# A two-layer encoder on one core: the last round of the feed-forward's second product over all tokens, and un-normed features for layer 1

## The chip, the cores and the metric

The kernel runs on one core of a Trainium2 chip. The metric is the device time of one execution in microseconds (us), the median of several. Five engines work beside each other: TensorE (PE, with weight loads PEld), VectorE (DVE), ScalarE (ACT), GpSimd (POOL) and SyncE (SP), which issues the DMAs.

## The reference, cut to what matters

Two groups of tokens (1024 of a new stream and 64 of a running one) share all weights, so the kernel has T = 1088 columns. Layer 0 has mixers A and B, layer 1 has C and D; behind each stands a squared-ReLU MLP. What the change touches is the MLP's second product, the norm that opens layer 1, layer 1's mixer and the final norm:

```
def trunk(x, ...):                         # D_MODEL 1024, D_FF 4096, two layers
    for layer in range(2):
        h = rms_norm(x, norm_mix_g[layer])
        y = even_mixer(h) if layer == 0 else odd_mixer(h)
        x = x + y
        h = rms_norm(x, norm_ffn_g[layer])
        x = x + square(relu(h @ w_ff1[layer])) @ w_ff2[layer]
    return rms_norm(x, final_norm_g)

def rms_norm(x, g):  return x * rsqrt(mean(x * x) + EPS) * g

def odd_mixer(h):
    z = h @ w_in
    c_in = z[:, :512] * sigmoid(z[:, 512:1024])
    c = silu(layer_norm(causal_dwconv(c_in, 31 taps) + bias))
    gate_b, gate_c, xt = z[:, 1024:1536], z[:, 1536:2048], z[:, 2048:]
    d = gate_b * causal_dwconv(gate_c * xt, 3 taps)
    return concat(c, d) @ w_out
```

## The kernel before, in words

Features lie on the 128 partitions, tokens along the columns. x is eight tiles X of 128 x 1088. The tokens are cut into two halves c = 0 and c = 1 of NH = 544 columns, each of two quarters of NQ = 272. Every fp32 operand is split into a rounded high part and a remainder (`split`, lines 164 to 166: an ACT copy, then a DVE subtraction), and every product takes three matmuls.

**Feed-forward.** Both products of the MLP use seven products of 2 x 2 block matrices in place of eight. `form` (line 197) makes the seven weight forms of one block: one load into RAW, four sums on DVE (line 212), seven splits into slots W, of which there are six. `take` and `ahead` (lines 234 and 220) make forms ahead of their use, in the order of a plan. The hidden features are stored in DRAM as seven forms each (`hd`), and `Hidden.form` loads and splits them back into tiles FA (c = 0) and FB (c = 1), four each.

The second product goes in steps (`STEPS2`, lines 333 to 336): a step multiplies for output block j the hidden blocks lo to hi, seven forms f, for the halves in cs; `products` (line 782) issues 7 x 3 matmuls per hidden block and half, and line 878 adds each form's PSUM result into X. In the last round hidden blocks 12 + j to 15 are multiplied for j = 0 to 3 (4, 3, 2, 1 blocks wide), first for c = 1, all four j, then for c = 0, all four j again:

```
STEPS2 += [(j, 12 + j, 16, (), (c,)) for c in (1, 0) for j in range(4)]
```

So the weight forms of these four steps are loaded and made twice. In this round the updated X is squared on ACT (lines 885 and 888, one square tile `sq`) and summed on POOL into acc (line 889).

**Norm and layer 1.** When a half is done, `done(c)` appends its norm to `beside`, a list from which `aside` takes two pieces after each form. In layer 0 that is `norm1` (line 900): `rms_half` (line 297: two sums on PE, a reciprocal root on ACT, three DVE steps, lines 305 to 308), then for each of the eight tiles a store of x to DRAM, a product with gain and factor on DVE (line 908) and a split into tiles h. For c = 1 these run beside the matmuls of c = 0; for c = 0 beside the first projections, which `conv_pairs` (line 1014) therefore issues for c = 1 first: gates and GLU inputs of pair 0 and the gate of pair 1 for c = 1, then c = 0.

`project` (line 957) multiplies one 128-row block of the input projection for both halves, 48 matmuls a half, into one of two PSUM pairs. A gate is emptied by a sigmoid on ACT (line 998), a GLU input by a DVE product (line 1002). `conv` (line 1046) lists the 31 taps of each of four channel blocks for DVE (line 1074, accumulating in PSUM) or, all 31 of block 0 and 18 of block 2, for POOL (line 1063, with ACT products); `some` (line 948) releases them at fixed rates after each half-projection. `short_conv` (line 1093) does the same for mixer D: gate_c is copied by ACT (line 1101), gate_x is a DVE product (line 1105), two taps on DVE (line 1116), gate_b a DVE product (line 1123) and a split into dd. The order in which an engine runs its instructions is not the source's: the framework that builds the program orders them itself.

**The end.** For layer 1 `finish(c)` (line 1202) scales the eight tiles of a half on ACT (line 1208), does `rms_half`, multiplies by the factor on DVE or POOL (line 1213) and stores the output. The pieces of c = 1 run beside c = 0's matmuls.

Of the kernel before, what the change touches and what calls it, by code (L numbers as in the profile page):

```python
# [16 lines left out]
P = 128  # L17
# [39 lines left out]
def encoder(ctx, tc, ins, outs):  # L57
# [29 lines left out]
    RIGHT = {"P1", "P2", "t", "raw", "FA", "vr", "sq", "RAW", "e", "cin", "dd", "wide", "yt"}  # L87
    LEFT = {"Q1", "Q2", "FB", "vl", "h", "cc"}
# [108 lines left out]
    def form(key, blocks):  # L197
# [99 lines left out]
    def rms_half(c, t):  # L297

        ps = pair()
# [32 lines left out]

    STEPS2 = [(2, 0, 2, (2,)), (3, 0, 3, (3,)), (1, 0, 1, ()), (0, 0, 4, (4,))]
    STEPS2 += [((w - 4) % 4, w - 4, w, (w,)) for w in range(5, 16)]
    STEPS2 = [(*s, (0, 1)) for s in STEPS2]
    STEPS2 += [(j, 12 + j, 16, (), (c,)) for c in (1, 0) for j in range(4)]

    def plan_ff(layer):
# [5 lines left out]
        for s, (j, a, b, _, _) in enumerate(STEPS2):  # L344
            src = ins[f"wf2_{layer}"][j, :, :, a * P : b * P].rearrange("b p c -> p b c")
            for f in range(7):
                plan(("f2", layer, s, f), src, "form")
# [422 lines left out]
    def feed_forward(layer, done):  # L770
# [10 lines left out]

        def products(key, cs, n, rows):
# [5 lines left out]
            for f, (name, first) in enumerate(  # L788
# [4 lines left out]
                w = take((*key, f), 5)  # L793
                for c in cs:
                    ps = bank[name][:, c, :NQ]
                    for q in range(n):
                        lh, ll = w[:, 0, q * P : q * P + P], w[:, 1, q * P : q * P + P]
                        t = FF[c, rows[q]][:, PLACE[f]]
# [6 lines left out]
                aside(2)  # L805

        class Hidden:
# [5 lines left out]
            def form(self, f):  # L813
                t = self.buffer()
                dma.dma_start(out=t, in_=hd[self.i][f])
                for c in range(2):
                    to = FF[c, self.i % 4][:, PLACE[f]]
                    split(to[:, 0], to[:, 1], t[:, c * NQ : c * NQ + NQ])

        factor = acc.rearrange("p (c h t) -> p c h t", c=2, h=2)  # L820
        for s, (i, cs) in enumerate(STEPS1):
# [4 lines left out]
            for f, ps in products(("f1", layer, s), cs, 4, range(4)):  # L826
# [45 lines left out]
        for s, (j, lo, hi, make, cs) in enumerate(STEPS2):  # L872
            nxt = [Hidden(i) for i in make]
            for f, ps in products(("f2", layer, s), cs, hi - lo, [k % 4 for k in range(lo, hi)]):

                m, h = ((j, 0), (j + 4, 1), (j, 1), (j, 0), (j + 4, 1), (j, 1), (j + 4, 0))[f]
                t = xv[m][:, cs[0] : cs[-1] + 1, h]
# [447 lines left out]
```

## Time and profile before

| | |
|---|---|
| median of 3 runs | 2128.63 us (2127.48 to 2131.05) |
| the profiled execution | 2128.48 us, span in the trace 2126.7 us |
| mean granted PE clock | 0.978 |
| PE busy | 2012.8 us (95%) |
| DVE busy | 1687.0 us (79%) |
| ACT busy | 993.7 us (47%) |
| POOL busy | 276.6 us (13%) |

Times in the trace are counted from the span's start. A window's row gives the busy time of each engine in it with the number of its instructions in brackets; PEclk is the granted clock of TensorE as a share of full speed. A row of lines groups equal instructions: count, busy us, mean ns, then the engine's idle time ahead of them and what ended it.

### The profile page before, as it was taken

To read this page: it belongs to the slowest core of one execution; us is meant where nothing else is said; L and a number is where in the kernel's file an instruction comes from. 1 tells how busy PE (TensorE), PEld (TensorE's weight loads), DVE (VectorE), ACT (ScalarE), POOL (GpSimd) and SP (SyncE) were. 2 spreads that over 40 slices of the span, in tenths; PEclk is the share of its full clock that TensorE was granted. 3 is DMA by queue.
4 is the path that set the end of the run, shared out by engine and by line. 5 is a ranking of instruction groups with operands and counts; after the bars stand their busy time and mean duration, and the time that the engine had idled before them with its cause. 6 is when DMAs were issued, how large, how long until landed. Compare 5 with 4: busy or idle time off the path is not lost.

```text
span 2126.7 us, 38667 instructions
## 1 busy us (share of the span) xinstructions
PE 2012.8 (95%) x15212; PEld 1975.0 (93%) x15212; DVE 1687.0 (79%) x2855; ACT 993.7 (47%) x1836; POOL 276.6 (13%) x204
## 2 busy tenths in 40 slices
PE   7999998999998999997899999979999989999995
PEld 5799998999998999997899999979999989999984
DVE  7785789676769988889579967998676779888887
ACT  6233555444445444444454425664343454444453
POOL 5200110000000000002166750300000000000023
PEclk9999999999999999998999999999999999999997
DMA  4223224434347445422211141234434466444412
GB/s 151 71 62 103 85 94 145 159 125 160 126 167 248 152 133 155 134 88 97 98 50 43 31 104 61 90 105 144 152 141 143 146 209 191 151 136 153 128 56 99
DMA packets 128406, 259.83 MB, mean 122 GB/s; under 512 B 16928, under 2 KB 38560, under 8 KB 123616
## 3 DMA queue, kind: packets, MB, share of 16 engines
q1 hardware_dynamic: 128224, 257.37, 37.1%
q8 instruction: 119, 1.95, 0.4%
q14 instruction: 63, 0.52, 0.1%
HBM read 185.69 MB, written 71.63 MB: 121 GB/s over the span
## 4 chain that ended last, share of the span: by engine, by line
PE 74%; DVE 16%; ACT 3%; issue 3%; POOL 2%; DMA 2%; DVEq 0%; SPq 0%; ACTq 0%; POOLq 0%
PE pp L801 19%; PE pp L803 18%; PE pp L802 18%; PE pp L248 4%; PE pp L249 4%; PE pp L250 4%; DVE W L166 2%; PE ps L248 2%; DVE ps L1074 2%; PE ps L249 2%; PE ps L250 2%; DVE X L878 1%; DMA vr<-hd 1%; DVE FB L166 1%; DVE Wl L166 1%
## 5 line engine op out<-in xcount | busy, mean ns | idle before, releaser
L801 PE MATMUL pp<-FA,W 128*128 128x272 f32 x1792 | 526.2, 295 | 45.6 <-DVE X L878 28.6
L801 PE MATMUL pp<-FB,W 128*128 128x272 f32 x1792 | 520.4, 290 | 16.4 <-DVE W L166 10.8
L802 PE MATMUL pp<-FA,W 128*128 128x272 f32 x1792 | 522.8, 292 | 0.1
L803 PE MATMUL pp<-FA,W 128*128 128x272 f32 x1792 | 522.2, 292 | 0.0
L803 PE MATMUL pp<-FB,W 128*128 128x272 f32 x1792 | 515.4, 288 | 0.0
L802 PE MATMUL pp<-FB,W 128*128 128x272 f32 x1792 | 515.3, 288 | 0.0
L801 PEld LDWEIGHTS pp<-FA,W 128*128 128x128 f32 x1792 | 344.0, 192 | 55.1 <-DVE X L878 32.2
L801 PEld LDWEIGHTS pp<-FB,W 128*128 128x128 f32 x1792 | 337.8, 188 | 20.5 <-issue 9.3
L802 PEld LDWEIGHTS pp<-FA,W 128*128 128x128 f32 x1792 | 345.9, 193 | 0.6 <-DVE FA L166 0.5
L803 PEld LDWEIGHTS pp<-FA,W 128*128 128x128 f32 x1792 | 343.4, 192 | 0.0
L802 PEld LDWEIGHTS pp<-FB,W 128*128 128x128 f32 x1792 | 341.3, 190 | 0.0
L803 PEld LDWEIGHTS pp<-FB,W 128*128 128x128 f32 x1792 | 337.9, 189 | 0.0
L166 DVE TENSOR_TENSOR W<-RAW,W 128x512 fp32r<-128x512 f32 (+3 forms) x356 | 234.4, 662 | 55.6 <-ACT W L165 54.7
L165 ACT ACTIVATE W<-RAW 128x512 fp32r<-128x512 f32 (+3 forms) x356 | 204.7, 582 | 136.1 <-PE pp L803 88.5
L889 POOL TENSOR_TENSOR acc<-acc,sq 128x272 f32<-128x272 f32 x56 | 47.9, 855 | 1387.7 <-ACT sq L888 1387.7
L165 ACT ACTIVATE W<-e 128x512 fp32r<-128x512 f32 (+3 forms) x246 | 143.3, 583 | 179.7 <-PE pp L803 116.6
L878 DVE TENSOR_TENSOR X<-X,pp 128x544 f32<-128x544 f32 (+1 forms) x322 | 197.5, 618 | 35.6 <-PE pp L803 33.4
L166 DVE TENSOR_TENSOR W<-e,W 128x512 fp32r<-128x512 f32 (+3 forms) x246 | 159.3, 647 | 67.5 <-ACT W L165 66.4
L248 PE MATMUL pp<-h,Wl 128*128 128x272 f32 x640 | 186.0, 291 | 5.2 <-DVE X L1105 3.3
L249 PE MATMUL pp<-h,Wh 128*128 128x272 f32 x640 | 185.5, 290 | 1.1 <-DVE h L166 1.1
L250 PE MATMUL pp<-h,Wh 128*128 128x272 f32 x640 | 185.8, 290 | 0.0
L1063 POOL TENSOR_TENSOR X<-X,X 128x1118 f32<-128x1118 f32 x46 | 126.6, 2751 | 94.1 <-ACT X L1061 91.6
(228 smaller groups left out, 3680.7 us busy)
## 6 DMA issues: line engine op xcount, KB each, us to landing
RAW<-in_wf SPq DMA_DIRECT2D x64, 1024.0 KB, 5.2
vr<-hd SPq DMA_DIRECT2D x119, 272.0 KB, 2.9
hd<-vl SPq DMA_DIRECT2D x105, 272.0 KB, 2.3
vl<-hd SPq DMA_DIRECT2D x105, 272.0 KB, 2.8
hd<-vr SPq DMA_DIRECT2D x91, 272.0 KB, 2.2
raw<-in_wi SPq DMA_DIRECT2D x18, 512.0 KB, 3.4
hd<-vl SPq DMA_DIRECT2D x42, 136.0 KB, 1.8
RAW<-in_wf SPq DMA_DIRECT2D x6, 768.0 KB, 4.5
```

What stands on the lines that cost most here:

```text
L165: act.activation(hi, src, AF.Copy)
L166: dve.tensor_tensor(lo, src, hi.bitcast(F32), ALU.subtract)
L248: pe.matmul(ps, ll, rh, start=s, stop=False)
L249: pe.matmul(ps, lh, rl, start=False, stop=False)
L250: pe.matmul(ps, lh, rh, start=False, stop=e)
L801: pe.matmul(ps, ll, hi, start=s, stop=False, skip_group_check=True)
L802: pe.matmul(ps, lh, lo, start=False, stop=False, skip_group_check=True)
L803: pe.matmul(ps, lh, hi, start=False, stop=e, skip_group_check=True)
L878: dve.tensor_tensor(t, t, ps, ALU.subtract if f in (1, 4, 6) else ALU.add)
L889: gp.tensor_tensor(at, at, sq, ALU.add)
L1063: return gp.tensor_tensor(o, o, t, ALU.add)
L1074: return dve.scalar_tensor_tensor(out=o, in0=z[:, k : k + NO], scalar=wk(k), in1=o, op0=ALU.mult, op1=ALU.add)
```

## The change

In layer 0 the last round takes both halves in each step, so its forms are made once. In layer 1 steps 0 and 1 take both halves; steps 2 and 3 take c = 1, then c = 0, and the second time use the forms that `kept` still holds. Narrow forms share a slot (`packed`: two of 256 columns, four of 128). After each step j of layer 0, `after` multiplies the rows j and j + 4 of x by the gain alone and splits them into the tile of FB that this step freed (`place` orders FB so) and one vl tile; x is stored whole. Layer 1's projections run on these features without the norm's factor r; `project` does `rms_half` behind its first two half-projections, keeps r in acc and r squared in r2, and r is multiplied in later: the gate by r before the sigmoid and by r after it, gate_c by r squared, the gated convolution by r. `conv_pairs` becomes a plain loop. In step 3 the squares are summed on DVE, in the others on POOL. `finish` scales x step by step.

```
@@ form, slots
-        w = wslot("W", [P, 2, 512])
-        split(w[:, 0:1, :n], w[:, 1:2, :n], (a11, e, e, a12, a11, e, a22)[f])
+        per = packed(n)
+        if f % per == 0:
+            four["w"] = wslot("W", [P, per, 2, 512 // per])
+        w = four["w"][:, f % per, :, :n]
+        split(w[:, 0:1], w[:, 1:2], (a11, e, e, a12, a11, e, a22)[f])
         return w
+    def packed(n):
+        return {P: 4, 2 * P: 2}.get(n, 1)
     def slots(src, kind):
-        return 2 if kind == "w" and src.shape[1] == 1024 else 1
+        if kind == "form":
+            return 1 / packed(src.shape[2])
+        return 2 if src.shape[1] == 1024 else 1
@@ steps of the second product
-    STEPS2 += [(j, 12 + j, 16, (), (c,)) for c in (1, 0) for j in range(4)]
+    ENDS = [
+        [(j, 12 + j, 16, (), (0, 1)) for j in range(4)],
+        [(j, 12 + j, 16, (), (0, 1)) for j in (0, 1)] + [(j, 12 + j, 16, (), (c,)) for c in (1, 0) for j in (2, 3)],
+    ]
@@ products, Hidden
-                w = take((*key, f), 5)
+                if (*key, f) not in kept:
+                    kept[(*key, f)] = take((*key, f), 5)
+                w = kept[(*key, f)]
+        def place(i, c):
+            return (3, 2, 0, 1)[i % 4] if c else i % 4
-                    to = FF[c, self.i % 4][:, PLACE[f]]
+                    to = FF[c, place(self.i, c)][:, PLACE[f]]
@@ feed_forward, second product
-        for s, (j, lo, hi, make, cs) in enumerate(STEPS2):
+        for j, lo, hi, make, cs in STEPS2 + ENDS[layer]:
...
                 dve.tensor_tensor(t, t, ps, ALU.subtract if f in (1, 4, 6) else ALU.add)
                 if hi == 16 and f >= 3:
-                    (c,) = cs
-                    t, at = xv[m][:, c, h], factor[:, c, h]
-                    if (c, h) not in started:
-                        started.add((c, h))
+                    at = factor[:, part, h]
+                    if (part.start, h) not in started:
+                        started.update((c, h) for c in cs)
                         act.activation(at, t, AF.Square)
                     else:
-                        sq = square_tile(NQ)
+                        sq = square_tile(len(cs) * NQ).rearrange("p (c t) -> p c t", t=NQ)
                         act.activation(sq, t, AF.Square)
-                        gp.tensor_tensor(at, at, sq, ALU.add)
+                        (dve if j == 3 else gp).tensor_tensor(at, at, sq, ALU.add)
...
-            if hi == 16 and j == 3:
-                done(cs[0])
+            if hi == 16:
+                done(j, cs)
@@ norm1 and after become
+    h1 = [[[None] * KT for _ in range(2)] for _ in range(2)]
+    def after(j, cs):
+        t = sb([P, 7, NH], F32R, "FB", 4)
+        places = [t[:, i] for i in range(7)] + [sb([P, NH], F32R, "vl", 4)]
+        def one(k, c):
+            a = c * NH
+            g, xk = col(O_G + 2 * KT + k), x[k][:, a : a + NH]
+            hi, lo = (h1[c][i][k] for i in range(2))
+            act.activation(hi, xk, AF.Copy, scale=g)
+            dve.scalar_tensor_tensor(out=lo, in0=xk, scalar=g, in1=hi.bitcast(F32), op0=ALU.mult, op1=ALU.subtract)
+        for c in (1, 0):
+            for k in (j, j + 4):
+                for i in range(2):
+                    h1[c][i][k] = places.pop()
+                beside.append(lambda k=k, c=c: one(k, c))
+        for k in (j, j + 4):
+            dma.dma_start(out=xd[k], in_=x[k])
     feed_forward(0, after)
+    aside(len(beside))
@@ project (its k in the order MS = 0, 4, 1, 5, 2, 6, 3, 7)
+            if unnormed:
+                assert unnormed.pop(0) == c
+                rms_half(c, wide(), psum3().rearrange("p (h t) -> p h t", h=3)[:, :2])
+                rr = halves(r2[:, c * NH : c * NH + NH])
+                dve.tensor_tensor(rr, r_of(c), r_of(c), ALU.mult)
             ps_of(c, ps[:, :, :NQ])
@@ gate
-            act.activation(halves(sg[c]), ps, AF.Sigmoid)
+            s = halves(sg[c])
+            dve.tensor_tensor(s, ps, r_of(c), ALU.mult)
+            act.activation(s, s, AF.Sigmoid)
+            dve.tensor_tensor(s, s, r_of(c), ALU.mult)
@@ conv_pairs: the hand-written order of pairs 0 and 1 goes
-        for j in (2, 3):
+        for j in range(4):
@@ short_conv
-            act.activation(halves(gc[c]), ps, AF.Copy)
+            dve.tensor_tensor(halves(gc[c]), ps, halves(r2[:, c * NH : c * NH + NH]), ALU.mult)
...
+            dve.tensor_tensor(halves(oc), halves(oc), r_of(c), ALU.mult)
             dve.tensor_tensor(halves(oc), halves(oc), ps, ALU.mult)
@@ finish
+        a, b = cs[0] * NH, (cs[-1] + 1) * NH
+        beside.extend([lambda k=k: scaled(k, a, b) for k in (j, j + 4)])
+        if j == 3:
+            (c,) = cs
+            beside.extend([lambda: rms_half(c, vs())] + [lambda k=k: one(k, c) for k in MS])
```

## Rows read from the trace of the kernel before

**Rows 1.** The page's first part: busy us (share of the span) xinstructions.

```profile
PE 2012.8 (95%) x15212; PEld 1975.0 (93%) x15212; DVE 1687.0 (79%) x2855; ACT 993.7 (47%) x1836; POOL 276.6 (13%) x204
```

**Rows 2.** Windows by stage; behind the colon length and PE, PEld, DVE, ACT, POOL.

```profile
1900.00:1920.00 20.00, 20.00 (x162) 20.00 (x161) 16.51 (x31) 8.96 (x20) 0.00 (x0) 1.00 0.47 149
940.60:970.90 30.30, 27.98 (x213) 26.64 (x211) 27.77 (x63) 14.50 (x36) 7.87 (x10) 1.00 0.36 119
970.90:1022.60 51.70, 36.77 (x217) 33.71 (x218) 47.74 (x94) 24.00 (x54) 13.79 (x15) 0.81 0.27 94
1022.60:1051.10 28.50, 27.39 (x198) 26.65 (x197) 16.72 (x29) 14.10 (x19) 3.18 (x4) 0.93 0.24 79
1075.00:1240.00 165.00, 159.76 (x1258) 158.92 (x1257) 159.10 (x132) 77.92 (x80) 115.37 (x44) 0.99 0.14 41
1240.00:1280.00 40.00, 40.00 (x316) 39.52 (x315) 22.11 (x32) 13.25 (x21) 16.25 (x11) 1.00 0.52 141
2034.40:2064.10 29.70, 26.67 (x203) 25.47 (x202) 26.88 (x63) 18.32 (x43) 8.51 (x11) 1.00 0.21 63
2064.10:2107.40 43.30, 33.35 (x217) 31.50 (x217) 40.14 (x82) 23.25 (x53) 15.32 (x16) 0.86 0.25 88
2107.40:2126.70 19.30, 2.29 (x5) 1.17 (x4) 8.78 (x10) 3.31 (x6) 5.77 (x5) 0.50 0.31 115
```

**Rows 3.** Waits of PE, 940.6 to 1051.1: us in total, times, longest.

```profile
PE pp L801 <- DVE X L878: 11.0, 11, 2.4
PE pp L303 <- POOL acc L889: 3.8, 1, 3.8
PE pp L801 <- DVE W L166: 2.4, 2, 2.2
```

**Rows 4.** Windows of DVE, tile W alone, in the round's second half.

```profile
970.90:1022.60 51.70, 13.93 (x27) 0.81 0.27 94
```

**Rows 5.** The same window of DVE, line 212 alone.

```profile
970.90:1022.60 51.70, 10.17 (x16) 0.81 0.27 94
```

**Rows 6.** Groups of DVE by form, 940.6 to 1051.1.

```profile
L878 DVE TENSOR_TENSOR X<-X,pp 128x272 f32<-128x272 f32 x56 | 23.2, 428 | 2.9 <-PE pp L803 2.8
L166 DVE TENSOR_TENSOR h<-vr,h 128x544 fp32r<-128x544 f32 x8 | 6.0, 746 | 0.0
...
L908 DVE SCALAR_TENSOR_TENSOR vr<-X,par,acc 128x544 f32<-128x544 f32 x8 | 5.9, 777 | 0.0
...
L878 DVE TENSOR_TENSOR X<-X,pp 128x544 f32<-128x544 f32 x1 | 0.7, 722 | 0.2 <-PE pp L803 0.2
```

**Rows 7.** Groups of the whole span: POOL's additions of 544 columns, PE's norm sums.

```profile
L739 POOL TENSOR_TENSOR acc<-acc,sq 128x544 f32<-128x544 f32 x28 | 43.3, 1546 | 290.4 <-ACT sq L738 290.4
...
L303 PE MATMUL pp<-acc,ones 128*128 128x272 f32 x32 | 10.7, 464 | 11.4 <-POOL acc L889 7.4 <-POOL acc L739 3.5 <-DVE vl L843 0.5
```

**Rows 8.** Groups of DVE by form, 1075 to 1240.

```profile
L166 DVE TENSOR_TENSOR dd<-X,dd 128x544 fp32r<-128x544 f32 x5 | 8.4, 1686 | 0.7 <-ACT dd L165 0.7
L1123 DVE TENSOR_TENSOR X<-X,pp 128x544 f32<-128x544 f32 x5 | 3.6, 714 | 0.1
```

**Rows 9.** Timeline of DVE, 1100 to 1175: start us, us, instruction [idle before].

```profile
1118.96 0.06 DVE L1096 MEMSET X<- 128x2 f32 x1
...
1123.52 0.72 DVE L1002 TENSOR_TENSOR cin<-pp,wide 128x544 f32<-128x544 f32 x1 [0.35 <-PE pp L250]
...
1160.71 0.71 DVE L166 TENSOR_TENSOR dd<-X,dd 128x544 fp32r<-128x544 f32 x1
...
1165.09 3.13 DVE L166 TENSOR_TENSOR dd<-X,dd 128x544 fp32r<-128x544 f32 x1
```

**Rows 10.** Groups of POOL, 1060 to 1280.

```profile
L1063 POOL TENSOR_TENSOR X<-X,X 128x1118 f32<-128x1118 f32 x46 | 126.6, 2751 | 94.1 <-ACT X L1061 91.6
```

**Rows 11.** Groups of DVE by form, 2034.4 to 2107.4: output products.

```profile
L1213 DVE TENSOR_TENSOR vr<-X,acc 128x544 f32<-128x544 f32 x6 | 6.5, 1103 | 0.0
```

**Rows 12.** Timeline of DVE, its last addition into X.

```profile
2107.55 0.44 DVE L878 TENSOR_TENSOR X<-X,pp 128x272 f32<-128x272 f32 x1 [0.46 <-PE pp L803]
```

**Rows 13.** Timeline of POOL, its last addition of squares.

```profile
2110.31 0.76 POOL L889 TENSOR_TENSOR acc<-acc,sq 128x272 f32<-128x272 f32 x1 [0.54 <-ACT sq L888]
```

More of the change, by code (lines that the diff above doesn't have):

```diff
@@ L295, in gain, with rms_half @@
         dve.scalar_tensor_tensor(out=lo, in0=x, scalar=g, in1=hi.bitcast(F32), op0=ALU.mult, op1=ALU.subtract)
-    def rms_half(c, t):
-        ps = pair()
+    def rms_half(c, t, ps=None):
+        ps = pair() if ps is None else ps
         a = c * NH
@@ L343, in plan_ff @@
                 plan(("f1", layer, s, f), src, "form")
-        for s, (j, a, b, _, _) in enumerate(STEPS2):
+        steps = {(j, a): b for j, a, b, _, _ in STEPS2 + ENDS[layer]}
+        for (j, a), b in steps.items():
             src = ins[f"wf2_{layer}"][j, :, :, a * P : b * P].rearrange("b p c -> p b c")
             for f in range(7):
-                plan(("f2", layer, s, f), src, "form")
+                plan(("f2", layer, (j, a), f), src, "form")
     plan_ff(0)
@@ L780, in feed_forward @@
         hd = [drp.tile([7, P, NH], F32, tag=f"hd{layer}_{i}", name=f"hd{layer}_{i}") for i in range(16)]
+        kept = {}
         def products(key, cs, n, rows):
@@ L825, in feed_forward @@
             z = {k: halves(vl() if last or s < 2 else vs()) for k in (0, 3, 1, 2)}
-            for f, ps in products(("f1", layer, s), cs, 4, range(4)):
+            for f, ps in products(("f1", layer, s), cs, 4, lambda q, c: q):
                 v = {k: t[:, cs[0] : cs[-1] + 1] for k, t in z.items()}
@@ L893, in feed_forward @@
                 begun.add(f"m{layer + 1}")
-            if hi == 16 and j == 3:
-                done(cs[0])
-    h1 = [None, None]
-    def norm1(c):
-        a = c * NH
-        t = vr if c == 1 else lambda: sb([P, NH], F32, "yt", 3)
-        def one(k):
-            y, xk = t(), x[k][:, a : a + NH]
-            dma.dma_start(out=xd[k][:, a : a + NH], in_=xk)
-            dve.scalar_tensor_tensor(
-                out=y, in0=xk, scalar=col(O_G + 2 * KT + k), in1=acc[:, a : a + NH], op0=ALU.mult, op1=ALU.mult
-            )
-            split(h1[c][0][k], h1[c][1][k], y)
-        return [lambda: rms_half(c, t())] + [lambda k=k: one(k) for k in MS]
-    def after(c):
-        if c == 1:
-            open_side("left")
-            for i in (0, 1):
-                h1[1 - i] = [[sb([P, NH], F32R, "h", 32) for _ in range(KT)] for _ in range(2)]
-            beside.extend([lambda: None] * 2)
-        beside.extend(norm1(c))
+            if hi == 16:
[17 more added lines that the diff above has]
+            dma.dma_start(out=xd[k], in_=x[k])
     feed_forward(0, after)
+    aside(len(beside))
     h = h1
@@ L955, in some, with r_of, project @@
                         q.pop(0)()
-    def project(key, ps_of, rates, order=(1, 0), w=None):
-        w = take(key) if w is None else w
-        for c in order:
+    def r_of(c):
+        return halves(acc[:, c * NH : c * NH + NH])
+    unnormed = [1, 0]
+    def project(key, ps_of, rates):
+        w = take(key)
+        for c in (1, 0):
             ps = pair()
@@ L1214, in one @@
             dma.dma_start(out=outs["yT"][k, :, a : a + NH], in_=y)
-        return [lambda k=k: scaled(k) for k in MS] + [lambda: rms_half(c, t())] + [lambda k=k: one(k) for k in MS]
-    feed_forward(1, lambda c: beside.extend(finish(c)))
+        a, b = cs[0] * NH, (cs[-1] + 1) * NH
[3 more added lines that the diff above has]
+            beside.extend([lambda: rms_half(c, vs())] + [lambda k=k: one(k, c) for k in MS])
+    feed_forward(1, finish)
     aside(len(beside))
```

45 lines of the change are left out of this document (13 added, 32 removed).

## Prediction

> **What bounds the kernel now.** I read the page's busy times first: PE is busy 2012.8 of 2126.7 us, DVE 1687 [rows 1]. A busy PE is not yet a PE at its rate, so next come the windows by stage, where the count of matmuls tells the rate [rows 2]: in the steady part of the second product 162 matmuls take 20.00 us, 0.1235 us each, and DVE has 3.5 us to spare. That is the yardstick. Beside it stand two bad places. The last round of layer 0's second product with the opening of layer 1 is the first three stretches after that row: 30.3 + 51.7 + 28.5 = 110.5 us. Their matmuls are 420 of the round and 192 of the first two projections, 612 x 0.1235 = 75.6 us, and two sets of four norm sums, 0.464 us each but overlapping [rows 7], which I put at 1.2 us a set: 78 us. So 32 us are lost there, most of them while the first half of the tokens is multiplied (c = 0), where DVE is busy 47.7 of 51.7 us and the granted clock is 0.81. The waits say the same: PE stands 11.0 us for the addition into X and 3.8 us for POOL's squares [rows 3]. The second bad place is the same round of layer 1 with the output: 29.7 + 43.3 + 19.3 = 92.3 us to the end of the span, for 51.9 us of matmuls. Between them, projections and convolutions (1075 to 1240) have DVE busy 159.1 of 165.0 us with PE almost at its rate: there DVE has no room, but from 1240 to 1280 it has 17.9 us [rows 2].
>
> **The round of layer 0.** Both halves now share one set of weight forms. The forms of one half cost DVE 13.9 us of splits [rows 4] and 10.2 us of sums [rows 5]; that goes. The 56 additions of 272 columns (0.428) become 28 of 544 (0.722): 24.0 to 20.2 us. The eight normalising products of that half (0.777 each, 6.2 us) and the norm's three steps (2.2) leave the round; the splits of the other half come in (8 x 0.746 = 6.0), and four squares of the last step move from POOL to DVE (two inputs in SBUF like that split: 2.9) [rows 6]. DVE's 75.5 us become 75.5 - 24.1 - 3.8 - 6.2 - 2.2 + 6.0 + 2.9 = 48.1, below PE's 51.9. The round then runs at PE's rate as a whole, but not at its end: steps j = 2 and 3 and the 18 matmuls that the next projection can do before it needs the last feature give PE 144 x 0.1235 = 17.8 us, while DVE has 14 additions (10.1), ten feature splits (7.5), four squares (2.9) and one or two weight splits of layer 1 (some 2.5), 23 us, and the chain addition, copy on ACT, split behind the last one is 2.5 us more. **I take 9 us of drain.** ACT is a cover here that can fail: one square tile serves all, so each square waits for POOL to have read the one before. At 544 columns a POOL addition takes 1.546 us [rows 7] where it now takes 0.76 [rows 13], so with the square itself each one in steps 0 to 2 holds ACT some 2.2 us, and feature copies queue behind it. That bounds the drain at 19 us (9 more, four squares of step 2 in full); below it is 3 (DVE's 23 fitted into earlier slack, only the last chain left).
>
> Layer 1 opens behind this: the norm is no longer waited for, since the first projections run on un-normed features and PE does the norm's sums between them; its chain (reciprocal root, three steps, the square of the factor, one product) is six instructions of some 0.7 us on ACT and DVE, 4 to 6 us with their hand-overs, and the second PSUM pair gives PE 48 x 0.1235 = 5.9 us meanwhile. I allow 1.5 us. The clock falls when PE idles: 0.93 in the opening stretch now, 28.5 x 0.07 x 2 = 4 us at the lower level (1.2 for 2.4 GHz), 2 us lost [rows 2]; with an idle time at a new place I take 3, between 0 and 5. Loss after: 9 + 1.5 + 3 = 13.5 for 32.5. **Gain 19 us** (8 to 26). On SP, eight writes of whole X tiles replace sixteen halves and one set of weight loads goes; the write of step 3 stands ahead of the load of the second unit of weights after it, which is needed two projections (24 us) later.
>
> **The added work in layer 1's mixer.** Un-normed features cost DVE in every projection but the GLU inputs and the x branch. Of each gate: a product from PSUM with the factor and, after the sigmoid, one in SBUF (16 in all); of gate_c: one from PSUM in place of an ACT copy (8); of gate_b: one more in SBUF (8). The first eight, of pairs 0 and 1, come before 1075, when no tap runs yet and DVE has holes (16.7 of 28.5 us busy in the opening [rows 2]); I cost them at nothing, and if that cover is gone they are 6 us. Left are 12 from PSUM at 0.714 (8.6 us) [rows 8] and 12 with both inputs in SBUF. The nearest row of those is the split of the short convolution, which in this stretch takes 1.686 us in the mean [rows 8] though it takes 0.71 alone and 3.13 at worst [rows 9]. What stretches it is POOL: its 46 additions take 2.75 us each [rows 10], and products that read PSUM keep their 0.71 beside them. Ten at 1.686 and the last two, behind POOL's work, at 0.71: 18.3. The sum is 27 us of DVE against 5.9 us of its idle time before 1240 and 17.9 behind it. Does work slide there? The trace says yes: DVE does not keep the source's order. A memset of the short convolutions runs at 1118.96, ahead of the last GLU product of the pairs at 1123.52, which stands before it in the source [rows 9]; taps fill holes. So 3 us don't fit, and evacuations that come late behind stretched products cost PE some 9 us now (165.0 us for 1258 matmuls, 155.4 at the rate [rows 2]); half as much again is 4 to 5, and I take 4. **Loss 7 us**, between 0 (all slides) and 27 (none does).
>
> **The round of layer 1 and the end.** Steps 0 and 1 take both halves, 294 matmuls, 36.3 us at PE's rate, with DVE below it. Then each half does steps 2 and 3 with kept forms, and from there DVE sets the pace: 28 additions of 272 columns (12.0), eight squares (3.4), the norm's steps of c = 1 (2.2), its six output products (6.5 [rows 11]), and 2.2 us in which step 2 of c = 1 still waits for PE: with the last square's wait 27 us. Behind the last addition there are now 18.7 us. POOL's last two squares, each waiting for the other's tile, end at 2111.07 [rows 13], 3.1 us after that addition [rows 12]; on DVE one square and one sum are 1.0. The rest, 4 sums on PE, the root and the norm's steps, products and output, stays: 16.6. The kept forms fill all six weight slots, so step 3's last forms come only when step 1's are done: 1 us. 36.3 + 27 + 16.6 + 1 = 81 for 92.3. **Gain 11.5 us** (5 to 16).
>
> Narrow forms now share a slot, so at the start of each second product more of them are made ahead, the same instructions earlier while DVE is full. I take nothing, with 3 us either way (the longest waits of PE for a form are of 2.2 [rows 3]).
>
> **Sum.** The profiled execution took 2128.5 us (span 2126.7 and 1.8 around it) and the median of the runs is 2128.6, so both are one baseline. 2128.5 - 19 + 7 - 11.5 = 2105.
>
> **Rivals.**
> *The evacuations are the new bound.* Gates were emptied by ACT; now DVE must do it behind queued taps. For it: DVE at 96% from 1075 to 1240. Against it: the 17.9 us behind. If only the 5.9 us inside the stretch help, the loss is 21, not 7: 2119.
> *The round stays held.* ACT's squares behind POOL keep the drain at 19 us and a few more: gain 8 instead of 19, 2116. For it: PE waits 3.8 us for POOL already [rows 3]; against it: the additions into X, which free PE, do not need ACT.
> *Slower: products that wait out POOL.* Place: the 12 products with both inputs in SBUF. If each ends like the 3.13 us split, they cost 37.6 and with the other 8.6 us 46; less 5.9 of idle time DVE makes the mixer 40 us longer. The gains are 30.5, so beyond that the change loses: 2138. For it: by their mean two of the five splits of that kind took about 3.1 [rows 8, 9]; against it: the other three took 0.71, and POOL is idle for 30% of that stretch [rows 2]. The Trainium skill (SBUF — State Buffer, Who interferes with whom) says that a VectorE instruction with two SBUF inputs and a GpSimd one that reads SBUF exclude each other for the whole instruction, the later one blocked. By that rule 0.71 and 3.13 (0.71 and most of a 2.75 us addition) are the two ends, as the trace has them, and which comes up depends on who starts first.
> *Better than that.* Drain 3 and no loss in the mixer: 2092.
>
> **Chances.** Forecast 0.53 (own range 2098 to 2112), evacuations 0.15, round held 0.15, slower 0.07, better 0.10. The range 2093 to 2122 leaves out the slower case, a third of the evacuations' and part of the better one. A measurement of this kernel can tell some 0.2% (4.3 us) from no change. Faster by more: 0.53 + 0.10 + 0.10 of the evacuations + 0.13 of the held round = 0.86; within it 0.04 + 0.02 = 0.06; slower 0.01 + 0.07 = 0.08.
>
> **What would show it.** Right: the round of layer 0 at some 62 us with its idle PE at steps 2 and 3 and at the first projection; no long wait of PE for POOL's squares at its end; products with the factor from PSUM at 0.71 us and those in SBUF between 0.7 and 3.1; DVE full from 1240 to 1280 of the old clock; the last addition some 10 us closer to its round's start. Wrong: the 24 us of forms gone and the round hardly shorter (then DVE's order or ACT held it); PE at its rate through the whole mixer (all slid), or over 15 us of waits there for the new products.

## The result, and the profile after

The changed kernel takes 2106.76 us (median of 4 runs, 2105.87 to 2109.33) for 2128.72 of the kernel before (4 runs): ratio 0.9896, 95% interval 0.9881 to 0.9911. The profiled execution took 2106.23 us with a span of 2104.4, 22.3 less than the span before. The prediction was 2105.

The page's busy times, the answer to [rows 1]: PE has the same instructions and DVE 100 fewer, yet DVE's share stays at 79%.

```profile
PE 2004.5 (95%) x15212; PEld 1969.6 (94%) x15212; DVE 1653.7 (79%) x2755; ACT 965.4 (46%) x1744; POOL 261.5 (12%) x172
```

Since both kernels issue the same number of matmuls, their time lines can be laid side by side by the count of matmuls. The windows below begin and end at the counts at which those of [rows 2] do: the round of layer 0 with the opening (three rows), the mixer of layer 1 (two), the round of layer 1 and the end (three).

```profile
938.20:964.70 26.50, 26.50 (x214) 26.50 (x213) 17.14 (x27) 10.50 (x19) 2.74 (x2) 1.00 0.17 63
964.70:1001.90 37.20, 30.52 (x218) 29.17 (x217) 32.61 (x55) 19.01 (x36) 11.49 (x8) 0.90 0.30 111
1001.90:1030.30 28.40, 27.02 (x199) 26.51 (x198) 16.04 (x28) 11.17 (x14) 0.00 (x0) 0.95 0.29 97
1054.20:1228.80 174.60, 161.63 (x1258) 160.09 (x1257) 168.75 (x153) 74.18 (x73) 119.49 (x44) 0.97 0.13 39
1228.80:1269.50 40.70, 40.70 (x315) 40.21 (x314) 22.27 (x36) 9.34 (x16) 10.60 (x9) 0.98 0.53 141
2018.80:2044.00 25.20, 25.20 (x204) 25.20 (x203) 13.62 (x23) 9.65 (x15) 2.75 (x2) 1.00 0.07 21
2044.00:2086.90 42.90, 31.75 (x221) 29.11 (x219) 34.95 (x71) 20.78 (x43) 16.14 (x14) 0.88 0.16 59
2086.90:2104.40 17.50, 2.15 (x4) 1.17 (x4) 9.16 (x12) 2.47 (x4) 3.63 (x2) 0.50 0.34 128
```

The round and opening take 92.1 us for 110.5: 18.4 gained. The mixer takes 215.3 for 205.0: 10.3 lost, of which 1 comes back behind it. The last round and the end take 85.6 for 92.3: 6.7 gained.

The waits of PE in these three places (us in total, times, longest), first the one that answers to [rows 3]; its waits for POOL's squares and for forms are gone:

```profile
PE pp L819 <- DVE X L901: 6.7, 5, 2.6
PE pp L257 <- DVE wide L1030: 1.4, 1, 1.4
...
PE pp L257 <- DVE X L1139: 10.4, 3, 5.9
PE pp L257 <- DVE X L1120: 2.3, 1, 2.3
...
PE pp L819 <- DVE X L901: 10.6, 6, 7.2
PE pp L312 <- DVE acc L911: 2.1, 1, 2.1
```

L1139 is the product that empties the last gate of a short convolution, the mixer's new wait. L901, the addition into X, holds PE once for 7.2 us close to the end.

The rest of the 22.3 us lies where I had set nothing. The table gives, for every kernel run, what its profiled execution gained (+) or lost on the kernel before, in us, between the same counts of matmuls (their starts in the time lines). Three steady stretches of -0.8 to +1.0 us each are left out.

| kernel | 0 to 4200: same code | 4200 to 4800: second product of layer 0 starts | 6600 to 7500: round and opening | 7500 to 9600: mixer | 12300 to 12900: second product of layer 1 starts | 14700 to end | span |
|---|---|---|---|---|---|---|---|
| changed | +1.3 | +1.5 | +18.4 | -9.3 | +5.1 | +6.7 | +22.3 |
| no sharing at start | +0.4 | +0.7 | +18.8 | -9.3 | +2.7 | +6.8 | +20.1 |
| rows in order | +2.2 | +1.5 | +18.7 | -9.4 | +2.6 | +7.2 | +21.7 |
| neither | +1.9 | +1.5 | +18.8 | -9.3 | +1.4 | +7.0 | +21.9 |
| no r | +1.7 | +3.0 | +21.0 | +0.2 | +4.2 | +7.3 | +37.2 |
| no r in SBUF | +1.7 | +0.7 | +18.3 | -4.8 | +4.8 | +7.1 | +27.2 |
| product first | +1.2 | +2.1 | +18.3 | -12.3 | +4.3 | +6.9 | +20.0 |
| rate 2.1 | +2.6 | +1.7 | +18.6 | -7.2 | +3.5 | +6.8 | +26.2 |
| halves | -1.0 | +3.2 | +17.0 | -9.6 | +2.9 | +7.3 | +19.5 |
| four square tiles | -1.4 | +1.6 | +22.2 | -9.6 | +4.8 | +9.4 | +26.6 |
| outputs behind | -1.2 | +2.1 | +18.2 | -9.5 | +3.9 | +10.9 | +24.4 |
| three together | +0.9 | +1.7 | +22.1 | -7.4 | +4.0 | +14.6 | +35.9 |
| taps moved | +0.9 | +1.9 | +22.0 | -7.1 | +4.4 | +14.8 | +36.7 |

The first column is a measure of chance: the code is the same in all thirteen, and single executions differ there by 4 us. Kernels whose code is the same in a later stretch agree there far better (round and opening 18.2 to 18.8, end 6.7 to 7.3). So in these two a stretch tells an edit of 2 us that a total hardly does. At the starts of the second products the same code spreads more widely, from 0.7 to 3.2 us in layer 0 and from 2.9 to 5.1 in layer 1, and all rows are held against one execution of the kernel before.

### The profile page after: what moved, and what is told of

Its sections match the earlier page's. It is cut to its first block, busy times and chain, and to the rows that moved or that the text cites. A ratio compares the mean times of both kernels' runs of the same rounds, so it can differ in the third digit from the quotient of the medians.

```text
span 2104.4 us, 38324 instructions
## 1 busy us (share of the span) xinstructions
PE 2004.5 (95%) x15212; PEld 1969.6 (94%) x15212; DVE 1653.7 (79%) x2755; ACT 965.4 (46%) x1744; POOL 261.5 (12%) x172
## 4 chain that ended last, share of the span: by engine, by line
PE 73%; DVE 17%; ACT 4%; issue 2%; POOL 2%; DMA 2%; DVEq 0%; SPq 0%; ACTq 0%; POOLq 0%
PE pp L819 19%; PE pp L821 19%; PE pp L820 19%; DVE ps L1089 4%; PE pp L257 4%; PE pp L258 3%; PE pp L259 3%; DVE W L166 2%; PE ps L257 2%; PE ps L258 2%; PE ps L259 2%; DVE Wl L166 1%; DVE X L901 1%; DMA vr<-hd 1%; DVE FB L166 1%
## 5 line engine op out<-in xcount | busy, mean ns | idle before, releaser
L819 PEld LDWEIGHTS pp<-FA,W 128*128 128x128 f32 x1792 | 339.8, 190 | 42.2 <-DVE X L901 30.5
L820 PEld LDWEIGHTS pp<-FA,W 128*128 128x128 f32 x1792 | 342.0, 191 | 1.9 <-DVE FA L166 1.9
L821 PEld LDWEIGHTS pp<-FA,W 128*128 128x128 f32 x1792 | 339.9, 190 | 0.0
L165 ACT ACTIVATE W<-RAW 128x512 fp32r<-128x512 f32 (+3 forms) x324 | 191.1, 595 | 147.3 <-PE pp L821 104.7
L166 DVE TENSOR_TENSOR W<-RAW,W 128x512 fp32r<-128x512 f32 (+3 forms) x324 | 216.3, 670 | 51.9 <-ACT W L165 51.2
L901 DVE TENSOR_TENSOR X<-X,pp 128x544 f32<-128x544 f32 (+1 forms) x280 | 191.4, 690 | 55.1 <-PE pp L821 52.5
L165 ACT ACTIVATE W<-e 128x512 fp32r<-128x512 f32 (+3 forms) x222 | 132.2, 596 | 161.2 <-PE pp L821 118.7
L911 POOL TENSOR_TENSOR acc<-acc,sq 128x544 f32<-128x544 f32 (+1 forms) x24 | 29.6, 1234 | 1367.2 <-ACT sq L910 1367.2
L166 DVE TENSOR_TENSOR W<-e,W 128x512 fp32r<-128x512 f32 (+3 forms) x222 | 146.0, 658 | 61.7 <-ACT W L165 61.1
L258 PE MATMUL pp<-FB,Wh 128*128 128x272 f32 x640 | 186.4, 291 | 0.0
L257 PE MATMUL pp<-FB,Wl 128*128 128x272 f32 x480 | 140.1, 292 | 3.8 <-DVE X L1120 2.3
L259 PE MATMUL pp<-FB,Wh 128*128 128x272 f32 x480 | 139.3, 290 | 0.0
```

The lines of the kernel that those rows point to most:

```text
L165: act.activation(hi, src, AF.Copy)
L166: dve.tensor_tensor(lo, src, hi.bitcast(F32), ALU.subtract)
L257: pe.matmul(ps, ll, rh, start=s, stop=False)
L258: pe.matmul(ps, lh, rl, start=False, stop=False)
L259: pe.matmul(ps, lh, rh, start=False, stop=e)
L819: pe.matmul(ps, ll, hi, start=s, stop=False, skip_group_check=True)
```

## The experiments

### The mixer: all products with r left out, and half of them

```diff
-            dve.tensor_tensor(s, ps, r_of(c), ALU.mult)
-            act.activation(s, s, AF.Sigmoid)
-            dve.tensor_tensor(s, s, r_of(c), ALU.mult)
+            act.activation(s, ps, AF.Sigmoid)
...
-            dve.tensor_tensor(halves(gc[c]), ps, halves(r2[:, c * NH : c * NH + NH]), ALU.mult)
+            act.activation(halves(gc[c]), ps, AF.Copy)
...
-            dve.tensor_tensor(halves(oc), halves(oc), r_of(c), ALU.mult)
```

> The mixer of layer 1 without the factor 1/rms: this leaves out the multiplications with r and r squared after the gates' products (24 products of 544 elements on DVE; two of the evacuations are ACT's again). Theory A: the loss of 10.4 us between the matmuls 7500 and 9300 is DVE's added work, and PE waits for the evacuations queued behind it: the time falls by about 10, to some 2096.5, and the waits of PE for the gate products of the short convolutions (10.4 us now) are mostly gone. Rival B: the loss comes from the plain order of the column blocks (the halves of the gates no longer come first), and stays: 2106.8 within 2.

(They are 32 products in all, not 24.) Measured: 2093.81 us, ratio 0.9845 (0.9823 to 0.9867). The mixer's loss is gone (+0.2 for -9.3); Theory A. The second kernel takes away only the 16 with both inputs in SBUF (after the sigmoid, and ahead of L1139):

> Of the products with r only the 16 with both inputs in SBUF are left out (after the sigmoid, and in the last gate of the short convolutions); the 16 that read PSUM stay. Leaving out all gave 14 us by the medians. Theory A, by the record's own prices (1.686 us of one with two inputs in SBUF, 0.714 of one from PSUM): the share of the 16 is about two thirds, so 8 to 10 us come back, ratio about 0.9855. Rival B, by the durations in the trace after (8 at 1.03 and 8 at 0.72 against 16 at 0.72: 13.6 of 25.1 us): a little over half, 6 to 8 us, ratio about 0.9865. Rival C: the evacuations from PSUM are what PE waits for, and the others are hidden: under 3 us, ratio 0.989.

Measured: 2102.18 us, ratio 0.9885 (0.9871 to 0.9900), 2.3 us by the two ratios; the mixer loses 4.8 for 9.3, so by the stretch these 16 cost 4.5 us and the 16 from PSUM the other 5. That is less than A and B say and more than C: the two kinds cost about the same. The groups of DVE in the changed kernel's mixer, 1054.2 to 1228.8 (count, busy us, mean ns), say why:

```profile
L1089 DVE SCALAR_TENSOR_TENSOR ps<-cin,par,ps 128x1118 f32<-128x1118 f32 x69 | 95.3, 1381 | 4.7 <-ACT ps L1068 3.8
L166 DVE TENSOR_TENSOR Wl<-raw,Wh 128x1024 fp32r<-128x1024 f32 x13 | 27.5, 2113 | 0.1
L1131 DVE SCALAR_TENSOR_TENSOR X<-X,par,X 128x1024 f32<-128x1024 f32 x6 | 9.7, 1625 | 0.0
L1131 DVE SCALAR_TENSOR_TENSOR X<-X,par,X 128x64 f32<-128x64 f32 x6 | 7.4, 1237 | 0.0
L1032 DVE TENSOR_TENSOR wide<-wide,acc 128x544 f32<-128x544 f32 x4 | 5.3, 1326 | 0.0
L166 DVE TENSOR_TENSOR dd<-X,dd 128x544 fp32r<-128x544 f32 x5 | 5.0, 994 | 0.7 <-ACT dd L165 0.7
L1116 DVE TENSOR_TENSOR wide<-pp,r 128x544 f32<-128x544 f32 x6 | 4.3, 717 | 0.0
...
L1138 DVE TENSOR_TENSOR X<-X,acc 128x544 f32<-128x544 f32 x6 | 4.0, 714 | 0.0
L1030 DVE TENSOR_TENSOR wide<-pp,acc 128x544 f32<-128x544 f32 x4 | 2.9, 718 | 0.0
```

The new products are L1030, L1032, L1116 and L1138: 16.5 us, of which the ten with both inputs in SBUF are 9.3. And the taps (L1089) are 69 in this stretch, as in the same stretch of the kernel before (its groups of DVE by form, 1075 to 1240):

```profile
L1074 DVE SCALAR_TENSOR_TENSOR ps<-cin,par,ps 128x1118 f32<-128x1118 f32 x69 | 95.5, 1383 | 2.9 <-ACT ps L1053 1.4
L166 DVE TENSOR_TENSOR Wl<-raw,Wh 128x1024 fp32r<-128x1024 f32 x13 | 22.8, 1757 | 0.2
L1116 DVE SCALAR_TENSOR_TENSOR X<-X,par,X 128x1024 f32<-128x1024 f32 x6 | 12.2, 2041 | 0.1
L1116 DVE SCALAR_TENSOR_TENSOR X<-X,par,X 128x64 f32<-128x64 f32 x6 | 10.2, 1704 | 0.5 <-ACT X L1114 0.5
```

They are all taps of this group that the kernel has, and none has moved behind. DVE is busy 168.75 us for 159.1 before and the stretch is 9.6 us longer; behind it DVE is busy 22.27 us for 22.11. The idle time there took nothing.

### The mixer: order and rate

Product first:

```diff
-            dve.tensor_tensor(halves(oc), halves(oc), r_of(c), ALU.mult)
             dve.tensor_tensor(halves(oc), halves(oc), ps, ALU.mult)
+            dve.tensor_tensor(halves(oc), halves(oc), r_of(c), ALU.mult)
```

> In the last gate of the short convolutions the product that reads PSUM comes first, and the one with r behind it; the same work in another order. Theory A: what holds PE is that the product with r (0.71 us) stands between the tap work and the evacuation: each of the 3 long waits is shorter by 0.7, about 2 us in all, to some 2104.7. Rival B: the queue of taps ahead sets the wait, and one place in it changes nothing: 2106.8 within 0.7.

Measured: 2109.87 us, ratio 0.9915 (0.9898 to 0.9932), and in the mixer 12.3 us lost for 9.3: worse than both theories. PE's wait for this evacuation does get shorter, 9.1 us for 10.4 from three waits, but the next one, L1116, now holds PE 2.0 us for 0.2, so that all its waits in the mixer are 12.4 us for 12.9. The 3 us lie where PE counts as busy: 236.39 us for 233.29 between matmuls 7500 and 9300, at a mean clock of 0.97 for 0.98. Why PE is slower there stays open.

Rate:

```diff
-    RP, RD, NP2 = (2.85, 1.65), (2.4, 1.65), 18
+    RP, RD, NP2 = (2.85, 1.65), (2.1, 1.65), 18
```

> The taps on DVE are let go at 2.1 instead of 2.4 for each half of a column block in the second part of the mixer: some 7 taps of 1.38 us, 10 us of work, move behind, into the 40 us from 1220 on in which DVE has 15 idle. Theory A: the loss of the mixer is too much work on DVE too early, and the idle time behind takes it: about 5 us less, ratio about 0.987. Rival B: the taps then end late, the norm of the convolution with them, and the output products that read it wait: 0 to 4 us more.

Measured: 2101.71 us, ratio 0.9883 (0.9866 to 0.9900). The mixer loses 7.2 us for 9.3, but not as Theory A has it, for no tap moved behind. The rows of the tap line in the kernel before, the changed one and this one (ns shortest, median and longest, first and last start) show all 69 started by 1223.5 in each, and up to matmul 8760 the mixer's instructions on DVE stand in the same order as in the changed kernel:

```profile
L1074 DVE SCALAR_TENSOR_TENSOR ps<-cin,par,ps x69: 1372/1386/1390, 1077.5 to 1219.0; 128x1118 f32<-128x1118 f32 x69
L1089 DVE SCALAR_TENSOR_TENSOR ps<-cin,par,ps x69: 1373/1382/1389, 1056.7 to 1223.5; 128x1118 f32<-128x1118 f32 x69
L1089 DVE SCALAR_TENSOR_TENSOR ps<-cin,par,ps x69: 1369/1380/1390, 1055.2 to 1219.8; 128x1118 f32<-128x1118 f32 x69
```

What moved is a part of the convolution's norm, which follows the taps. It now runs between matmuls 9300 and 9600, where DVE had room (the changed kernel, then this one):

```profile
1300.65:1338.34 37.69, 37.69 (x303) 37.69 (x302) 22.44 (x34) 14.34 (x25) 5.09 (x4) 1.00 0.21 64
1296.99:1334.69 37.70, 37.70 (x302) 37.70 (x301) 30.33 (x53) 25.11 (x45) 5.08 (x4) 1.00 0.19 63
```

So 7.9 us of DVE's work did slide into idle time, for a gain of 2 us. The waits of PE in the mixer (1052.5 to 1266.5) show that the wait for L1139 is shorter, not gone:

```profile
PE pp L257 <- DVE X L1139: 8.3, 3, 3.8
PE pp L257 <- DVE X L1120: 2.3, 1, 2.3
```

### The start of the second product

No sharing at the start (the forms of the last round still share):

```diff
-    def packed(n):
-
-        return {P: 4, 2 * P: 2}.get(n, 1)
+    def packed(n, key):
+
+        start = key[0] == "f2" and key[2][1] == 0
+        return 1 if start else {P: 4, 2 * P: 2}.get(n, 1)
...
```

> The changed kernel, but the narrow forms at the start of the second product (steps that begin at row 0) take a slot each again; those of the last round still share. Theory A: sharing gives the gain that the two traces show at the same count of matmuls around the start of the second products (1.6 us in layer 0, 5 us in layer 1, where I had set 0): the time goes up by about 6.6, from 2106.8 to some 2113, and PE waits there as it did before the change. Rival B: the slots only happen to stand there, and the gain comes from the order of the rows or from what an earlier stage left: no change, 2106.8 within 1.

Measured: 2108.3 us, ratio 0.9914 (0.9893 to 0.9935): no rise by 6.6. At the starts it gains 0.7 and 2.7 us. The ten kernels that have sharing and new places in layer 1 gain 2.9 to 5.1 there, 4.2 in the mean. The next candidate was the new places:

```diff
-            return (3, 2, 0, 1)[i % 4] if c else i % 4
+            return (3, 2, 0, 1)[i % 4] if c and layer == 0 else i % 4
```

> In layer 1 the forms of the hidden rows of both halves take the same four places again (as before the change); layer 0 keeps the new places for c=1. The first run showed that sharing of slots isn't what shortens the start of layer 1's second product by some 5 us. Theory A: the new places are (a form is written over the rows that the first product reads last, and not first): the 5 us go, the ratio to the kernel before goes from 0.990 to some 0.992 (about 2112 on the scale of 2106.8), and PE again waits for about 5 us at the count of matmuls 12300 to 12900. Rival B: the wait of the kernel before came from when its transfers landed in that execution: no change, within 1 us, and the gain at that count stays between 4 and 6.5 us.

Measured: 2109.24 us, ratio 0.9917 (0.9902 to 0.9932); at the start of layer 1's second product 2.6 us are left, between A and B. So both were undone at once:

> Both parts undone at the start of the second product: no sharing of slots there, and in layer 1 the hidden rows in their old places. Between the matmuls 12300 and 12900 the changed kernel gains 3.6 to 5.1 us over the kernel before (eight runs), 2.7 without the sharing and 2.6 without the new places. Theory A: the two are separate causes and add up: 0 to 1.5 us left. Rival B: both act on the same wait, and one undone already costs all that the pair costs: 2 to 3 us left, from another cause.

Measured: 2106.64 us in a single run; 1.4 us are left at that start, as Theory A has it. Together sharing and places are worth about 2.8 of the 4.2 us there, each kernel being seen in one execution. Each alone stands only just below the spread of the kernels that have both, so how the 2.8 divide stays open, and so does the cause of the 1.4, which may be chance in the one execution of the kernel before. PE's longest wait there for the addition into X goes the same way: 5.0 us before, 3.9 with neither, 3.1 and 3.2 with one of the two, 2.8 in nine of the ten kernels with both (3.4 in the tenth). The windows of that start, of the kernel before, the changed one and the one with neither, show the same matmuls (602 or 603) with less idle time and a clock that falls less:

```profile
1710.60:1797.80 87.20, 79.86 (x603) 78.67 (x602) 76.54 (x164) 45.27 (x113) 0.00 (x0) 0.94 0.66 213
```

```profile
1699.80:1781.90 82.10, 76.79 (x602) 75.45 (x601) 77.14 (x166) 46.84 (x114) 0.00 (x0) 1.00 0.67 229
```

```profile
1697.24:1783.04 85.80, 79.13 (x603) 77.83 (x601) 76.65 (x163) 45.49 (x114) 0.00 (x0) 0.96 0.66 216
```

### The round: width and squares

Halves (in layer 0, steps j = 2 and 3 of the last round by halves, as in layer 1):

```diff
-        [(j, 12 + j, 16, (), (0, 1)) for j in range(4)],
         [(j, 12 + j, 16, (), (0, 1)) for j in (0, 1)] + [(j, 12 + j, 16, (), (c,)) for c in (1, 0) for j in (2, 3)],
-    ]
+    ] * 2
...
     def after(j, cs):
+        if cs == (1,):
+            return
```

> The changed kernel, but the last two steps (j = 2 and 3) of layer 0's last round go by halves again, with the forms kept, as layer 1's do; their un-normed features come after the second half. Theory A: what the round gained it gained from the width: 14 additions of 544 columns (10.1 us on DVE) become 28 of 272 (12.0), the squares likewise, and the last features and the norm sums all come behind the last half: of the 18.6 to 19.8 us that the runs gain between the matmuls 6600 and 7200, 13 to 16 are left, ratio about 0.992. Rival B: the width is of no matter, and the gain is that no forms are made twice and that the norm is no longer waited for: within 1 us of the changed kernel. Rival C: halves spread the additions better (one half's squares and sums lie beside the other's products), and the stretch gets shorter by 1 to 3 us.

Measured: 2109.06 us, ratio 0.9915 (0.9898 to 0.9931). Of 18.4 us 17.0 are left. In the stretch that the expectation names, to matmul 7200, 16.3 of 18.8 are left, just above the 13 to 16 of Theory A and too few for B. The width of the last two steps, with the features and sums that come later without it, is worth some 2 us; the rest is the forms that are no longer made twice, the first two steps and the norm that is no longer waited for, which these runs don't separate.

Four square tiles:

```diff
-                        sq = square_tile(len(cs) * NQ).rearrange("p (c t) -> p c t", t=NQ)
+                        sq = vr(len(cs) * NQ).rearrange("p (c t) -> p c t", t=NQ)
```

> The squares of the last round take turns in four buffers and no longer wait for the one square tile. Theory A: the additions to the sum of squares on POOL are in no one's way, the drain of layer 0's last round is the evacuations alone: within 1 us. Rival B (the record's rival that the round stays held by ACT and POOL squares): ACT waits for POOL (1.6 us at a time after the change), and evacuations and splits behind it on ACT wait too: 3 to 6 us less, between the matmuls 6600 and 7200 and in the last round of layer 1.

Measured: 2100.96 us, ratio 0.9878 (0.9862 to 0.9894). Rival B: 3.8 us more in round and opening (22.2 for 18.4) and 2.7 at the end. The totals alone would hardly tell: the ratios differ by 3.8 us and their intervals overlap. In the changed kernel ACT's waits from 938.2 to 1030.3 hold this row, which the kernel with four tiles no longer has:

```profile
ACT sq L910 <- POOL acc L911: 3.6, 5, 1.6
```

PE's wait of 1.4 us in the opening (L1030) goes with it: in the changed kernel a weight split of 1.22 us stands on DVE between the norm's factor (L317) and L1030, and with four tiles that split runs earlier, in DVE's wait for the norm.

### The end

Outputs behind:

```diff
-            beside.extend([lambda: rms_half(c, vs())] + [lambda k=k: one(k, c) for k in MS])
+            ones_ = [lambda k=k: one(k, c) for k in MS]
+            beside.extend(held[:5] + [lambda: rms_half(c, vs())] + held[5:])
+            if c == 1:
+                held.extend(ones_)
+            else:
+                beside.extend(ones_)
```

> The eight output products of the second half (c=1) of the last layer are held back until the last additions of the first half (c=0) are done: five ahead of its norm, three behind. Theory A: ahead of those additions they cost PE the wait of 7.2 us at 2075.6; the products then fall into the 7 us in which DVE waits for the norm of the first half: 5 us less, some 2101.8, and 2107 less the wait if nothing else comes up. Rival B: they lengthen the path behind the last addition by what they cost ahead of it (6 on DVE at 0.72 to 1.2 us): 2106.8 within 1.

Measured: 2103.43 us, ratio 0.9886 (0.9869 to 0.9904); the end gains 10.9 us for 6.7. Theory A. What it removes is seen in DVE's time line of the changed kernel (start, us, instruction):

```profile
2073.83 0.98 DVE L317 SCALAR_TENSOR_TENSOR acc<-vl,acc 128x544 f32<-128x544 f32 x1
2074.74 0.42 DVE L901 TENSOR_TENSOR X<-X,pp 128x272 f32<-128x272 f32 x1
2075.08 2.80 DVE L1228 TENSOR_TENSOR vr<-X,acc 128x544 f32<-128x544 f32 x2
2077.81 1.27 DVE L1228 TENSOR_TENSOR vl<-X,acc 128x544 f32<-128x544 f32 x1
2079.00 1.91 DVE L1228 TENSOR_TENSOR vr<-X,acc 128x544 f32<-128x544 f32 x2
2080.83 1.85 DVE L1228 TENSOR_TENSOR vl<-X,acc 128x544 f32<-128x544 f32 x1
2082.60 1.12 DVE L901 TENSOR_TENSOR X<-X,pp 128x272 f32<-128x272 f32 x3
```

and in PE's time line:

```profile
2083.08 0.94 PE L819 MATMUL pp<-FA,W 128*128 128x272 f32 x2 [7.22 <-DVE X L901]
```

As soon as c = 1's factor is there (L317), six output products run in a row for 7.5 us, ahead of the additions that would free PSUM for c = 0's last step.

### Together

> Three edits together, each of which was run alone: the output products held back, four square tiles, taps on DVE at 2.1. Theory A: they act in different stretches and add up. At the same count of matmuls the runs gave 4.1 us in the tail (held back), 2.1 in the last round of layer 0 and 2.6 in the tail (square tiles; of that 1 beside the first), 2.0 in the mixer (rate): 9 us less than the changed kernel, ratio to the kernel before about 0.985. Rival B: in the tail the squares and the held outputs now take the same four buffers and wait for each other, and the tail gives only what the better of the two gave: 8 us or less, ratio 0.986 to 0.987, with waits for vr tiles behind the last additions.

Measured: 2092.56 us (2091.59 to 2093.74), ratio 0.9835 (0.9822 to 0.9849), below the changed kernel's interval (0.9881 to 0.9911): faster than both kernels, by some 13 and 35 us. Theory A, and more than the 9 us that it expected; at the end the gain is even above the sum (14.6 for 6.7; the two alone gave 4.2 and 2.7 more). The windows of the end, to be held against the last two of the changed kernel's: the stretch to the last addition takes 33.9 us for 42.9, and the part behind it only 1.1 more.

```profile
2038.30:2072.20 33.90, 30.38 (x218) 28.12 (x216) 27.02 (x66) 20.17 (x43) 13.62 (x13) 0.97 0.07 25
2072.20:2090.80 18.60, 2.15 (x4) 1.17 (x4) 13.18 (x17) 1.97 (x4) 5.38 (x3) 0.50 0.56 211
```

The last kernel adds to these three NP2 = 21 and the rate 1.9:

> The same with three more taps of the third group on POOL (21 instead of 18) and the rate on DVE at 1.9. Theory A: the mixer is bound by what DVE has to do between the evacuations: three taps less are 4.1 us, and the rate moves more behind; between the matmuls 7800 and 9600 the loss against the kernel before falls from 9.3 us (7.3 with the rate 2.1) to 3 to 5; ratio 2 to 4 thousandths... that is 3 us better than the run beside it, some 0.9835. Rival B: POOL, which has 46 taps of 2.8 us in that stretch, ends late by 3 taps (8.5 us), the group's last tap on DVE waits for it and the norm behind waits too: no better or worse than the run beside it.

Measured: 2092.18 us, ratio 0.9834 (0.9820 to 0.9847): Rival B's number, no different; the mixer loses 7.1 us for 7.4. Between matmuls 7500 and 9600 DVE is busy 3.3 us less (241.02 for 244.31), yet the stretch is only 0.4 us shorter (282.25 for 282.62), and PE now waits 3.9 us for the evacuation L1116 in one piece. DVE's time line shows why, and it is Rival B's mechanism: the addition that joins POOL's taps to DVE's waits 8.40 us for POOL, and L1116 stands behind it.

```profile
1236.17 1.23 DVE L1100 TENSOR_TENSOR cin<-cin,X 128x1024 f32<-128x1024 f32 x1 [8.40 <-POOL X L1078]
1237.32 0.28 DVE L1095 SCALAR_TENSOR_TENSOR cin<-cin,par,ps 128x64 f32<-128x64 f32 x1
1237.63 0.89 DVE L1100 TENSOR_TENSOR cin<-cin,X 128x64 f32<-128x64 f32 x1
1238.43 0.71 DVE L1116 TENSOR_TENSOR wide<-pp,r 128x544 f32<-128x544 f32 x1
```

## Why the prediction was right, and where it was not

The total came out within 2 us, but three terms were off by 3 to 7 us and cancelled: that it came so close is luck.

**The round of layer 0 and the opening: 19 predicted, 18.4 measured.** The round takes 63.7 us where I said some 62, with DVE at 49.75 for my 48.1. Of the loss that stays (92.1 - 78 = 14.1 for 13.5) the parts differ: PE's wait in the opening is 1.4 us for 1.5, the clock costs 37.2 x 0.10 + 28.4 x 0.05 = 5.1 for 3 (its mean stands at 0.90 and 0.95 where PE waits between steps), and the drain is the remaining 7.6 for 9, with PE's 6.7 us of waits for L901 in it. The prediction's own terms for the drain, 23 - 17.8 + 2.5, give 7.7, and its upper bound, 9 and four times 2.2, is 18 and not 19. Reckoned alike, the clock cost 51.7 x 0.19 + 28.5 x 0.07 = 11.8 us before, and PE's waits fell from the 17.2 us of [rows 3] to 8.1; the two together are an estimate of 15.8 of the 18.4 us. The rival that ACT is held by POOL's squares has the right mechanism at a smaller price: it is worth 3.8 us, inside the drain and the opening, and not the 11 that I gave it.

**The mixer: loss of 7 predicted, 10.3 measured (9.3 up to matmul 9600).** The step that failed is "Does work slide there? The trace says yes". One memset that runs early showed that the order is not the source's; it didn't show that the taps move into the idle time. All 69 still run ahead of it, and the 17.9 us behind took nothing. What ties the taps to their place stays open: a lower rate left them there, though it moved the norm that follows them. My rival of the evacuations as the new bound was nearer in kind: PE waits 10.4 us for L1139. It overstated the price, as I did the work: ten products with both inputs in SBUF were to cost 1.686 us each and cost 0.93 in the mean. Lower work and no sliding nearly cancelled.

**The slower rival fell** by the durations. In the changed kernel's mixer nine of the ten new products with both inputs in SBUF take 0.72 us or less (L1138 stands in pairs of 1.34 to 1.35) and one 3.15:

```profile
1087.97 0.72 DVE L1032 TENSOR_TENSOR wide<-wide,acc 128x544 f32<-128x544 f32 x1
...
1091.96 3.15 DVE L166 TENSOR_TENSOR Wl<-raw,Wh 128x1024 fp32r<-128x1024 f32 x1
1095.03 3.15 DVE L1032 TENSOR_TENSOR wide<-wide,acc 128x544 f32<-128x544 f32 x1
```

POOL's time line at that place:

```profile
1088.73 17.31 POOL L1078 TENSOR_TENSOR X<-X,X 128x1118 f32<-128x1118 f32 x6 [4.26 <-ACT X L1076]
```

The nine short ones run where POOL has no addition in hand, as the first of these does in POOL's 4.26 us of idle time; the split and the L1032 behind it start while POOL adds, and each takes 3.15. The Trainium skill (SBUF — State Buffer, Who interferes with whom) says that issue order decides who blocks. The trace agrees: these two come after an addition has started, and they are the ones that wait. I had carried the mean of another line over to the new products; but the price goes with when an instruction starts, and it moves between lines. The weight splits pay more of it (2113 ns for 1757, 4.7 us in all), the splits of dd pay less (994 for 1686 [rows 8], 3.4 us), and so do the short convolution's own taps, the same twelve instructions with L1131 at 17.1 us where L1116 of before had 22.4.

**The round of layer 1 and the end: 11.5 predicted, 6.7 measured.** DVE's work was sized nearly right: it is busy 26.30 us in the 31.8 from the end of step 1 (2018.8 + 36.3 = 2055.1) to the last addition, where I had 27 with 2.2 of waiting in them. The step that failed is "from there DVE sets the pace". It does in the middle only:

```profile
2055.10:2075.10 20.00, 17.11 (x120) 15.39 (x118) 15.68 (x37) 11.28 (x22) 6.45 (x8) 1.00 0.00 1
2075.10:2082.60 7.50, 0.64 (x3) 0.42 (x3) 7.50 (x7) 2.36 (x4) 6.46 (x5) 0.61 0.49 186
2082.60:2086.90 4.30, 2.90 (x9) 2.19 (x9) 3.12 (x10) 1.35 (x4) 0.00 (x0) 0.50 0.53 196
```

Before and behind the block of outputs DVE waits for PE or ACT, within it PE waits for DVE. I had added up DVE's work as if its order did not matter. Holding the outputs back and giving the squares more tiles brings 7.9 us, which is more than the missing 4.8. Behind the last addition 17.5 us are left for my 16.6.

**Narrow forms: 0 predicted (3 either way), 1.5 and 5.1 measured.** The step that failed is "I take nothing": I priced the sharing of slots by the waits of layer 0's round and didn't look at the starts of the second products at all, nor at the new places. In this execution the kernel before loses 87.2 - 603 x 0.1235 = 12.7 us at layer 1's start, up to 0.06 x 87.2 = 5.2 of it by the clock, which stood at 0.94 there and at 1.00 in the changed kernel. With the same code there the kernel of the lower rate stood at 0.96, so part of the 5.1 may be chance.

**Not of the change:** 1.3 of the 22.3 us lie where the code is the same, within the 4 us by which executions differ there.

## What to carry to other kernels

Idle time behind a full stretch is worth something only if the work really moves there: see in a trace which instructions run ahead of it and which behind before counting on it. A lower release rate here left every tap ahead of it and moved other work. Work that is ready early on an engine that others wait for is not filler: hold it back until the instructions that free PSUM are issued. Where two kernels issue the same matmuls, compare them stretch by stretch at equal counts; errors that cancel in the total show there.

## What the runs showed that was not expected

Taking a buffer conflict off ACT (one square tile to four) gave 6.5 us in two places, although ACT is busy only 46% of the span. Taking an instruction out of an evacuation's way shortened PE's wait for it by 1.3 us and made the mixer 3 us longer. A single execution wanders by up to 4 us in its first 617 us, with the same code.
